# Layer norms in two passes on VectorE, and an output projection block by block with all weights on chip

## The chip, the core and the metric

One core of a Trainium2 chip runs the kernel. The metric is device time in microseconds, from the median of the runs. A core has TensorE (matmuls and transposes, results in eight PSUM banks), VectorE, ScalarE, GpSimd, and SyncE, whose queue issues all the transfers of this kernel.

## The reference, cut to what matters

One layer over 1024 tokens of width 1024: a mixer (forgetting attention and a gated linear recurrence, each projected to the full width, gated and added), its output projection, a residual with a layer norm, a SwiGLU FFN of hidden width 2816, and a second residual with a layer norm.

```python
merged = sigmoid(gate_a) * p_a + sigmoid(gate_b) * p_b
mix = merged @ w_o
x = layer_norm(ALPHA * x + mix, ln1_g, ln1_b)
u, g = split(x @ w_ff_in)
x = layer_norm(ALPHA * x + (silu(g) * u) @ w_ff_out, ln2_g, ln2_b)
# layer_norm(x, g, b) = (x - mean) * rsqrt(var + eps) * g + b, all in float32
```

## The kernel before, in words

Every float32 operand of a large matmul is split in two parts, high (`act.copy`, a cast on ScalarE) and low (`dve.tensor_sub` on VectorE; `split`), and `mm3` makes three matmuls of a product: high x high, high x low, low x high. A stationary tile has 128 x 128 elements, a moving one 128 x 512.

*The order of the work.* No engine's order is written by hand. Every call is first put down by `Plan.add`, with what it reads and writes; `Plan.schedule` then walks through time with a table of costs (`cost`, `LAT`), and gives each free engine the call that can start first, among equals the one with the lowest rank (the order of the calls; `plan.early` lowers a rank by `EARLY` = 3000). `issue` emits that order. A tile of a tag takes one of the tag's `BUFS` buffers as soon as one is free, in the order of first use (tags in `LOOSE` in any order). So each engine runs a fixed queue that was worked out from costs, and a call that comes late on the chip holds up what is queued behind it.

*Buffers.* `x`: five of 16 KB a partition (first the input, then the merged activations `mh`, `ml` of both token halves, then FFN operands). `wr0`, `wr1`: one raw weight load each, used in turn. `wh0`, `wl0`, `wh1`, `wl1`: two each, for split weights. `kb`, `pf`: four each (`REST` is these eight). `ph`, `tt`: four, `gt`: two, all of 512 elements a partition.

*Merge.* For each of 8 column blocks the second branch's product (banks `pps`) is gated, added, and split into `mh`, `ml`.

*Output projection.* The first 512 output columns go over all 8 token blocks at once, in eight banks (`o_acc`), one contraction row c after the other, with weights as they come. Then `z[t] = ALPHA * x + acc`, and the weights of the other 512 columns (`wo1`) are split into `REST`. For these, each token block t has its 24 matmuls (bank `o`), eviction, statistics (`stats`), and its layer norm.

*Layer norm* (`layer_norm`, `affine`). Mean and variance from `bn_aggr`; `rstd` by a power on GpSimd; `nmr` on VectorE; one pass a half on ScalarE (z * rstd + nmr); then the multiplication by g and the addition of b, on the engines that `engs` names ("d" VectorE, "p" GpSimd): "dp" in the first norm, "pp" and "dp" in the second. Only the very last block has its norm in two VectorE passes a half, in the branch `st is not None`.

*Transposes.* Eight transposes a block (`x1t`) make the FFN's operands X11, X12 (blocks 0 to 3) and X22, with copies r1, r2 (blocks 4 to 7).

*FFN.* Both products are formed from seven products of quarter matrices (p1 to p7; Winograd's form), on sums of operands: S1 to S4 on the token side, made by VectorE and ScalarE from r1 and r2 after the loop over blocks, and sums of weight quarters (`Chunk.sums`). Chunks 0 and 1 go product by product together (banks fa to fd), since S1 to S4 are made meanwhile; from chunk 2 on each goes by itself. Raw weights of a chunk come into `pf`.

*Second FFN product.* Six products over all groups, then p3 token block by token block, with its `ds` groups (weights `dbp`, activations `dap`, split into `dp`) kept on chip. Blocks 4 to 7 are complete after p7 and are normed beside p2; blocks 0 to 3 after p3.

Of the kernel before, what the change touches and what calls it, by code (L numbers as in the profile page):

```python
# [283 lines left out]
def trunk(ctx: ExitStack, tc, a: dict, out: bass.AP):  # L284
# [568 lines left out]
    def layer_norm(t, gb, engs, st=None, out=None):  # L853
# [6 lines left out]
        if st is not None:  # L860
            for hf in range(2):
                zt = z[t][:, hs(hf)]
                dve.scalar_tensor_tensor(zt, zt, mv[:, 0:1], gb[0][hf], op0=ALU.subtract, op1=ALU.mult)
            for hf in range(2):
                zt = z[t][:, hs(hf)]
                dve.scalar_tensor_tensor(zt, zt, rstd, gb[1][hf], op0=ALU.mult, op1=ALU.add)
                if out is not None:
                    sync.dma_start(out[:, hs(hf)], zt)
            return None
        nmr = small([P, 1], "nmr")  # L870
        dve.tensor_scalar(nmr, mv[:, 0:1], rstd, -1.0, op0=ALU.mult, op1=ALU.mult)
        for hf in range(2):
            zt = z[t][:, hs(hf)]
            act.activation(zt, zt, AF.Identity, bias=nmr, scale=rstd)
        return lambda: affine(t, gb, engs, out)

    def affine(t, gb, engs, out):
        for hf in range(2):
            zt = z[t][:, hs(hf)]
            e = [dve if x == "d" else pool for x in engs]  # L880
            e[0].tensor_mul(zt, zt, gb[0][hf])
            e[1].tensor_add(zt, zt, gb[1][hf])
            if out is not None:
                sync.dma_start(out[:, hs(hf)], zt)

    acc = [bank(ALL[t], f"o_acc{t}") for t in range(NT)]
    for c2 in range(KC // 2):
        w = weights(a["w_o"][0, c2], [2, NB], f"wo{c2}")
        for j in range(2):
            c = 2 * c2 + j  # L890
            for t in range(NT):
                lh, ll = mtok(t, c)
                mm3(acc[t], lh, ll, *w[j], c == 0, c == KC - 1)
    for t in range(NT):
        zt = z[t][:, hs(0)]
        dve.scalar_tensor_tensor(zt, zt, ALPHA, acc[t], op0=ALU.mult, op1=ALU.add)
    wo1 = []
    for c2 in range(KC // 2):
        raw = raw_load(a["w_o"][1, c2], [2, NB], f"wo1_{c2}")
        wo1.append([take(REST[2 * c2 + j], [2, NB], f"wo1{'hl'[j]}{c2}", F32R) for j in range(2)])  # L900
# [400 lines left out]
```

## Time and profile before

| | us |
|---|---|
| median of 3 runs | 1496.17 (1495.97 to 1496.75) |
| profiled execution, its own time | 1496.65 |
| its span, first to last instruction | 1494.9 |
| TensorE busy in the span | 1470.2 (98%) |
| VectorE busy | 998.2 (67%) |
| ScalarE busy | 671.5 (45%) |
| GpSimd busy | 156.2 (10%) |
| mean granted TensorE clock | 0.995 of full |

The profile is one execution recorded on the chip. Times in it are us from the start of the span, means of a group are in ns. A row of a timeline gives start, duration, engine, line, operation, output <- inputs, and in brackets how long the engine was idle before it and what ended that. Since all calls are emitted from one place, every row has line L280, and a reader goes by the names of the tiles. Matmuls are pipelined: a 512 wide one shows 0.39 us, while the next starts 0.23 us after it. PE is TensorE, PEld its weight loads, DVE VectorE, ACT ScalarE, POOL GpSimd, SPq SyncE's queue. The granted clock of 1.00 is TensorE's upper level (2.4 GHz), 0.50 its lower one (1.2 GHz).

### The profile page before, as it was taken

The numbers are of one execution on the slowest core, as the hardware profiler recorded it, in microseconds if no ns is written. First come the engines' busy times: TensorE is split into PE (matmuls) and PEld (weight loads), VectorE is DVE, ScalarE is ACT, GpSimd is POOL, SyncE is SP. The second block draws the span as 40 slices with busy tenths as digits, with TensorE's granted clock in tenths as the row PEclk, the third lists the DMA queues.
The fourth block names the chain that finished last, engine by engine and source line by source line (L and its number), as shares of the span: only waits on it lengthen the run. The fifth ranks groups of instructions, "written<-read, shape, count | busy, mean of one in ns | idle before, by whom it ended". The sixth has DMA issues, their size and how long they took to land.

```text
span 1494.9 us, 19370 instructions
## 1 busy us (share of the span) xinstructions
PE 1470.2 (98%) x7081; PEld 1218.2 (81%) x7081; DVE 998.2 (67%) x1890; ACT 671.5 (45%) x1133; POOL 156.2 (10%) x156
## 2 busy tenths in 40 slices
PE   9999999999999999999999899999999999999997
PEld 7987888888888888888887678888888888888885
DVE  5148676677797871135827998766666666798594
ACT  5127666677667743234512543332333333534341
POOL 0004132120100000000003300000000000000075
PEclk9999999999999999999999999999999999999998
DMA  7202212121211214347520124332232326977631
GB/s 245 73 29 83 75 47 78 54 60 40 82 37 52 78 59 154 106 163 255 182 69 0 57 86 136 101 100 97 98 100 101 102 104 200 338 271 242 225 118 71
DMA packets 78414, 170.67 MB, mean 114 GB/s; under 512 B 7400, under 2 KB 20328, under 8 KB 78320
## 3 DMA queue, kind: packets, MB, share of 16 engines
q1 hardware_dynamic: 78320, 169.44, 33.9%
q8 instruction: 56, 0.92, 0.2%
q14 instruction: 38, 0.31, 0.1%
HBM read 130.32 MB, written 39.09 MB: 113 GB/s over the span
## 4 chain that ended last, share of the span: by engine, by line
PE 72%; issue 17%; DVE 6%; POOL 2%; ACT 1%; DMA 0%; DVEq 0%; POOLq 0%; ACTq 0%
PE fb L280 12%; PE p L280 12%; PE fc L280 8%; PE fa L280 8%; PE bps L280 8%; PE gps L280 5%; PE va_acc L280 3%; PE vb_acc L280 3%; PE kps L280 3%; PE pv L280 2%; PE qps L280 2%; PE pt L280 2%; PE s L280 2%; POOL z L280 2%; PE lp L280 1%
## 5 line engine op out<-in xcount | busy, mean ns | idle before, releaser
L280 PE MATMUL p<-dp 128*128 128x512 f32 (+1 forms) x957 | 212.1, 384 | 3.9 <-DVE dp L280 3.9
L280 PEld LDWEIGHTS p<-dp 128*128 128x128 f32 x957 | 176.2, 189 | 39.9 <-DVE dp L280 4.2
L280 PE MATMUL fb<-xs,Tp 128*128 128x512 f32 x528 | 127.2, 389 | 0.7 <-DVE xs L280 0.4
L280 PE MATMUL fc<-xs,Tp 128*128 128x512 f32 x528 | 127.6, 389 | 0.0
L280 PE MATMUL fa<-x,Tp 128*128 128x512 f32 x504 | 122.2, 390 | 0.7 <-ACT p L280 0.7
L280 PEld LDWEIGHTS fb<-xs,Tp 128*128 128x128 f32 x528 | 98.9, 188 | 22.0 <-DVE xs L280 0.9
L280 PEld LDWEIGHTS fc<-xs,Tp 128*128 128x128 f32 x528 | 99.1, 188 | 21.0 <-ACT Tp L280 0.4
L280 PEld LDWEIGHTS fa<-x,Tp 128*128 128x128 f32 x504 | 94.6, 188 | 20.7 <-ACT p L280 1.2
L280 ACT CAST Tp<-t 128x512 fp32r<-128x512 f32 x88 | 54.2, 620 | 113.9 <-PE fc L280 65.6
L280 PE MATMUL gps<-xl,wg_h 128*128 128x512 f32 x256 | 101.3, 396 | 0.0
L280 PE MATMUL gps<-xh,wg_h 128*128 128x512 f32 x256 | 101.2, 395 | 0.0
L280 DVE TENSOR_TENSOR Tp<-t,Tp 128x512 fp32r<-128x512 f32 x88 | 60.7, 690 | 60.3 <-ACT Tp L280 59.9
L280 PE MATMUL gps<-xh,wg_l 128*128 128x512 f32 x256 | 100.7, 394 | 0.0
L280 POOL TENSOR_TENSOR rstd<-ve,mhalf 128x1 f32<-128x1 f32 x16 | 11.7, 730 | 825.0 <-DVE ve L280 824.0
L280 ACT CAST dp<-dap 128x1024 fp32r<-128x1024 f32 (+1 forms) x42 | 41.1, 982 | 90.9 <-PE p L280 40.3
L280 PE MATMUL bps<-xh,wb_l 128*128 128x512 f32 x192 | 76.0, 397 | 0.0
L280 PE MATMUL bps<-xh,wb_h 128*128 128x512 f32 x192 | 75.9, 396 | 0.0
L280 PE MATMUL bps<-xl,wb_h 128*128 128x512 f32 x192 | 75.9, 395 | 0.0
L280 DVE TENSOR_TENSOR tl<-pt,th 128x512 fp32r<-128x512 f32 (+1 forms) x96 | 50.7, 552 | 20.3 <-ACT th L280 20.0
L280 DVE TENSOR_TENSOR dp<-dap,dp 128x1024 fp32r<-128x1024 f32 (+1 forms) x42 | 51.8, 1235 | 16.1 <-ACT dp L280 16.0
L280 POOL TENSOR_SCALAR p<-p,rs 128x128 f32<-128x128 f32 (+3 forms) x64 | 47.8, 753 | 140.5 <-DVE rs L280 92.0
L280 DVE TENSOR_TENSOR wg_l<-wg_r,wg_h 128x512 fp32r<-128x512 f32 x32 | 22.5, 703 | 57.6 <-ACT wg_h L280 57.6
(287 smaller groups left out, 3414.1 us busy)
## 6 DMA issues: line engine op xcount, KB each, us to landing
dbp<-in_w_fo SPq DMA_DIRECT2D x45, 512.0 KB, 5.2
dap<-a_d SPq DMA_DIRECT2D x35, 512.0 KB, 4.7
wu_r<-in_w_ff SPq DMA_DIRECT2D x22, 512.0 KB, 3.6
wg_r<-in_w_ff SPq DMA_DIRECT2D x22, 512.0 KB, 3.5
a_d<-ar SPq DMA_DIRECT2D x42, 256.0 KB, 3.4
a_d<-as SPq DMA_DIRECT2D x33, 256.0 KB, 2.8
wg_r<-in_w_g SPq DMA_DIRECT2D x16, 512.0 KB, 3.7
gate_d<-gt SPq DMA_DIRECT2D x32, 256.0 KB, 2.4
```

What stands on the lines that cost most here:

```text
L280: getattr(q.engine, method)(*args, **kw)
```

## The change

The form of layer norm that the last block had becomes the only one: (z - mean) * g, then * rstd + b, four SCALAR_TENSOR_TENSOR a block on VectorE; ScalarE and GpSimd (but for the power) no longer take part. The output projection takes both column halves of a token block together: all weights `wo` of both halves are loaded and split at its start (rows 0 and 1 into the fifth `x` buffer, 2 and 3 into `wh`/`wl`, the rest into `REST`); blocks 0 to 2 run together, row by row, in six banks, and blocks 3 to 7 one after the other, half by half. The sums for S1 and the updates of r1, r2 move into the loop over blocks (for block 7 behind it). The raw weights of chunks 0 and 1 load into an `x` buffer instead of `pf`; their first two products have rank `EARLY`. The second norm's statistics get a tile of their own.

```diff
--- before
+++ after
@@ -850,58 +850,51 @@
     def stats(t, hf):
         dve.bn_stats(lnst[:, t, hf, :], z[t][:, hs(hf)])
 
-    def layer_norm(t, gb, engs, st=None, out=None):
+    def layer_norm(t, gb, st=None, out=None):
         mv = small([P, 2], "mv")
         dve.bn_aggr(mv, (lnst[:, t] if st is None else st).rearrange("p a b -> p (a b)"))
         ve = small([P, 1], "ve")
         dve.tensor_scalar(ve, mv[:, 1:2], LN_EPS, None, op0=ALU.add)
         rstd = small([P, 1], "rstd")
         pool.tensor_tensor(rstd, ve, mhalf[:, :1], op=ALU.pow)
-        if st is not None:
-            for hf in range(2):
-                zt = z[t][:, hs(hf)]
-                dve.scalar_tensor_tensor(zt, zt, mv[:, 0:1], gb[0][hf], op0=ALU.subtract, op1=ALU.mult)
-            for hf in range(2):
-                zt = z[t][:, hs(hf)]
-                dve.scalar_tensor_tensor(zt, zt, rstd, gb[1][hf], op0=ALU.mult, op1=ALU.add)
-                if out is not None:
-                    sync.dma_start(out[:, hs(hf)], zt)
-            return None
-        nmr = small([P, 1], "nmr")
-        dve.tensor_scalar(nmr, mv[:, 0:1], rstd, -1.0, op0=ALU.mult, op1=ALU.mult)
         for hf in range(2):
             zt = z[t][:, hs(hf)]
-            act.activation(zt, zt, AF.Identity, bias=nmr, scale=rstd)
-        return lambda: affine(t, gb, engs, out)
-
-    def affine(t, gb, engs, out):
+            dve.scalar_tensor_tensor(zt, zt, mv[:, 0:1], gb[0][hf], op0=ALU.subtract, op1=ALU.mult)
         for hf in range(2):
             zt = z[t][:, hs(hf)]
-            e = [dve if x == "d" else pool for x in engs]
-            e[0].tensor_mul(zt, zt, gb[0][hf])
-            e[1].tensor_add(zt, zt, gb[1][hf])
+            dve.scalar_tensor_tensor(zt, zt, rstd, gb[1][hf], op0=ALU.mult, op1=ALU.add)
             if out is not None:
                 sync.dma_start(out[:, hs(hf)], zt)
 
-    acc = [bank(ALL[t], f"o_acc{t}") for t in range(NT)]
-    for c2 in range(KC // 2):
-        w = weights(a["w_o"][0, c2], [2, NB], f"wo{c2}")
+
+    gb1 = lnrow("ln1_g", "ln1_b")
+    wo = {}
+
+    def wo_load(hf, c2, hi, lo):
+        raw = raw_load(a["w_o"][hf, c2], [2, NB], f"wo{hf}_{c2}")
+        if isinstance(hi, list):
+            for j in range(2):
+                split(hi[j], lo[j], raw[:, j])
+        else:
+            split(hi, lo, raw)
         for j in range(2):
-            c = 2 * c2 + j
-            for t in range(NT):
-                lh, ll = mtok(t, c)
-                mm3(acc[t], lh, ll, *w[j], c == 0, c == KC - 1)
-    for t in range(NT):
-        zt = z[t][:, hs(0)]
-        dve.scalar_tensor_tensor(zt, zt, ALPHA, acc[t], op0=ALU.mult, op1=ALU.add)
-    wo1 = []
-    for c2 in range(KC // 2):
-        raw = raw_load(a["w_o"][1, c2], [2, NB], f"wo1_{c2}")
-        wo1.append([take(REST[2 * c2 + j], [2, NB], f"wo1{'hl'[j]}{c2}", F32R) for j in range(2)])
-        split(*wo1[c2], raw)
-    for t in range(NT):
-        stats(t, 0)
-    gb1 = lnrow("ln1_g", "ln1_b")
+            wo[hf, 2 * c2 + j] = tuple(x[j] if isinstance(x, list) else x[:, j] for x in (hi, lo))
+
+    wx = take("x", [4, 2, NB], "wox", F32R)
+    for hf in range(2):
+        wo_load(hf, 0, wx[:, 2 * hf], wx[:, 2 * hf + 1])
+    for hf in range(2):
+        wo_load(hf, 1, *([half(f"w{x}{hf}", f"wo{hf}_{x}{j}", F32R) for j in range(2)] for x in "hl"))
+    for c2 in range(2, KC // 2):
+        for hf in range(2):
+            wo_load(hf, c2, *(take(REST[4 * c2 + 2 * hf + j - 8], [2, NB], f"wo{hf}_{'hl'[j]}{c2}", F32R)
+                              for j in range(2)))
+    OTAGS = ("s", "s", "s", "h", "h", "pv")
+    accs = [[bank(OTAGS[(2 * t + hf) % 6], f"o{hf}_{t}") for hf in range(2)] for t in range(NT)]
+
+    def wo_mm(t, hf, c):
+        lh, ll = mtok(t, c)
+        mm3(accs[t][hf], lh, ll, *wo[hf, c], c == 0, c == KC - 1)
 
 
 
@@ -917,14 +910,20 @@
         return ap.rearrange("p (c t) -> p c t", t=P)
 
     for t in range(NT):
-        o = bank("gh"[t % 2], f"o1_{t}")
-        for c in range(KC):
-            lh, ll = mtok(t, c)
-            mm3(o, lh, ll, wo1[c // 2][0][:, c % 2, :], wo1[c // 2][1][:, c % 2, :], c == 0, c == KC - 1)
-        zt = z[t][:, hs(1)]
-        dve.scalar_tensor_tensor(zt, zt, ALPHA, o, op0=ALU.mult, op1=ALU.add)
-        stats(t, 1)
-        layer_norm(t, gb1, "dp" if t < NT - 1 else "dd")()
+        if t == 0:
+            for c in range(KC):
+                for i in range(3):
+                    for hf in range(2):
+                        wo_mm(i, hf, c)
+        elif t > 2:
+            for hf in range(2):
+                for c in range(KC):
+                    wo_mm(t, hf, c)
+        for hf in range(2):
+            zt = z[t][:, hs(hf)]
+            dve.scalar_tensor_tensor(zt, zt, ALPHA, accs[t][hf], op0=ALU.mult, op1=ALU.add)
+            stats(t, hf)
+        layer_norm(t, gb1)
         s_ = blk(t % 4)
         tps = []
         for g in range(2):
@@ -938,13 +937,27 @@
         if t < 4:
             continue
         if t == 4:
-            X22 = operand("x", "x22")
+            X22, S1 = operand("x", "x22"), operand("x", "xs1")
             r2s = [take(f"wr{i}", [2, NB], f"r2s{i}") for i in range(2)]
         r1, r2 = (by4(x) for x in (half(("ph", "tt")[t % 2], f"r1_{t}"), r2s[t // 2 - 2][:, t % 2, :]))
         act.copy(r1, tps[0])
         split(X22[0][:, :, s_], X22[1][:, :, s_], tps[1])
         act.copy(r2, tps[1])
+
+        def first_sums(s_=s_, r1=r1, r2=r2, t=t):
+            s1 = by4(half("gt", f"s1r{t}"))
+            dve.tensor_add(s1, r1, r2)
+            split(S1[0][:, :, s_], S1[1][:, :, s_], s1)
+
+        def next_sums(s_=s_, r1=r1, r2=r2):
+            dve.tensor_sub(r1, f(X11[0])[:, :, s_], r1)
+            dve.tensor_add(r1, r1, f(X11[1])[:, :, s_])
+            dve.tensor_sub(r2, r2, r1)
+
         late.append((s_, r1, r2))
+        if t < NT - 1:
+            first_sums()
+            next_sums()
 
 
 
@@ -961,12 +974,15 @@
 
     TSLOTS = ("kb", "kb", "kb", "kb", "wr0", "wr1")
 
-    def stationary(src, name, apart=False):
+    lane01 = [0]
+
+    def stationary(src, name, apart=False, plain=False):
         if apart:
-            hi, lo = (take(f"w{x}0", [4, P], name + x, F32R) for x in "hl")
+            hi, lo = (take(f"w{x}{lane01[0]}", [4, P], name + x, F32R) for x in "hl")
+            lane01[0] ^= 1
         else:
-            t = take(TSLOTS[turns["T"] % len(TSLOTS)], [2, 4, P], name, F32R)
-            turns["T"] += 1
+            t = take("kb" if plain else TSLOTS[turns["T"] % len(TSLOTS)], [2, 4, P], name, F32R)
+            turns["T"] += not plain
             hi, lo = t[:, 0], t[:, 1]
         split(hi, lo, src)
         return hi, lo
@@ -978,9 +994,9 @@
             mm3(o, T[0][:, c], T[1][:, c], A[0][:, c], A[1][:, c], first and c == 0, c == 3, more)
 
     class Chunk:
-        def __init__(self, c):
+        def __init__(self, c, raw=None):
             self.c = c
-            self.g, self.u = (take("pf", [KC, P], f"w{n}{c}_r") for n in "gu")
+            self.g, self.u = raw or (take("pf", [KC, P], f"w{n}{c}_r") for n in "gu")
             for i, t in enumerate((self.u, self.g)):
                 sync.dma_start(t, a["w_ff"][c, i])
             self.r = {}
@@ -994,9 +1010,10 @@
                 dve.tensor_sub(self.r[n], x, y)
 
         def T(self, n, apart=False):
+            plain = self.c < 2
             src = {"p1": self.g[:, :4], "p2": self.g[:, 4:], "p3": self.u[:, 4:], "p4": self.r.get("4"),
                    "p5": self.r.get("1"), "p6": self.r.get("2"), "p7": self.r.get("3")}[n]
-            return stationary(src, f"T{n}_{self.c}", apart)
+            return stationary(src, f"T{n}_{self.c}", apart, plain)
 
     OPS = {"p1": X11, "p2": X12, "p4": X22}
     ars = {}
@@ -1052,32 +1069,30 @@
         activations(c, a0, a1)
 
 
-    ks = [Chunk(c) for c in range(2)]
+    first_sums()
+    plan.early = EARLY
+    raws = take("x", [4, KC, P], "w01_r")
+    ks = [Chunk(c, (raws[:, 2 * c], raws[:, 2 * c + 1])) for c in range(2)]
     banks = [[next_bank(f"f{n}{c}") for n in "abcd"] for c in range(2)]
     for k, o in zip(ks, banks):
         mul(k, "p1", o[0], True, True)
         k.p1 = half("ph", f"p1_{k.c}")
         act.copy(k.p1, o[0])
     for k, o in zip(ks, banks):
-        mul(k, "p2", o[0], False)
+        mul(k, "p2", o[0], False, True)
         k.sl = half("gt", f"sl{k.c}")
         act.activation(k.sl, o[0], AF.Silu)
-    S1 = OPS["p5"] = operand("x", "xs1")
-    for s_, r1, r2 in late:
-        S1r = half("wh1", "s1r")
-        dve.tensor_add(by4(S1r), r1, r2)
-        split(S1[0][:, :, s_], S1[1][:, :, s_], by4(S1r))
+    plan.early = 0
+    OPS["p5"] = S1
     for k, o in zip(ks, banks):
         k.sums("1", "2")
         mul(k, "p5", o[2], True)
         k.sums("4")
         mul(k, "p4", o[3], True)
+    next_sums()
     S3 = OPS["p7"] = operand("x", "xs3")
     S2 = OPS["p6"] = operand("x", "xs2")
     for s_, r1, r2 in late:
-        dve.tensor_sub(r1, f(X11[0])[:, :, s_], r1)
-        dve.tensor_add(r1, r1, f(X11[1])[:, :, s_])
-        dve.tensor_sub(r2, r2, r1)
         split(S2[0][:, :, s_], S2[1][:, :, s_], r2)
     for k, o in zip(ks, banks):
         mul(k, "p6", o[1], True)
@@ -1143,6 +1158,7 @@
     u = [half(("wh0", "wl0", "wh1", "wl1")[i], f"fu{i}") for i in range(4)]
     ai = {"p1": 0, "p5": 1, "p6": 2, "p7": 3, "p4": 4, "p2": 5, "p3": 6}
     gb2 = lnrow("ln2_g", "ln2_b")
+    lnst = take("gt", [NT, 2, 6], "lnst2")
     XS = ("x",) * 5
     for prod in ("p1", "p5", "p6", "p4", "p7", "p2"):
         if prod == "p7":
@@ -1178,14 +1194,13 @@
                 dve.tensor_add(z21, z21, u[t])
                 for hf in range(2):
                     stats(t + 4, hf)
-                layer_norm(t + 4, gb2, "pp", None, out[blk(t + 4), :])()
+                layer_norm(t + 4, gb2, None, out[blk(t + 4), :])
             else:
                 dve.tensor_add(z11, z11, o)
                 if t < 3:
                     stats(t, 0)
     ds = [group("p3", ai["p3"], g) for g in range(len(GR))]
     st = take("gt", [4, 6], "lnst3")
-    before = None
     for t in range(4):
         final = t == 3
         parts = [slice(i * 256, (i + 1) * 256) for i in (2, 3)] if final else [hs(1)]
@@ -1205,10 +1220,7 @@
                 dve.bn_stats(st[:, 2 + i, :], z[t][:, s_])
         if not final:
             stats(t, 1)
-        after = layer_norm(t, gb2, "pp" if t < 2 else "dp", st if final else None, out[blk(t), :])
-        if before:
-            before()
-        before = after
+        layer_norm(t, gb2, st if final else None, out[blk(t), :])
     plan.issue(SLACK, SWITCH)
```

## Rows read from the trace of the kernel before

**Rows 1.** The page's busy time of each engine: us, share of the span, instructions.
```profile
PE 1470.2 (98%) x7081; PEld 1218.2 (81%) x7081; DVE 998.2 (67%) x1890; ACT 671.5 (45%) x1133; POOL 156.2 (10%) x156
```

**Rows 2.** Busy time of each engine by stretch, then TensorE's clock, DMA share, GB/s.
```profile
400.00:500.00 100.00, 97.51 (x515) 81.71 (x513) 82.35 (x169) 67.26 (x105) 6.16 (x5) 1.00 0.18 56
...
790.00:840.00 50.00, 48.59 (x230) 37.69 (x229) 36.73 (x69) 18.35 (x29) 21.54 (x18) 1.00 0.01 2
840.00:860.00 20.00, 14.18 (x56) 10.67 (x55) 19.66 (x34) 14.65 (x24) 4.95 (x4) 0.83 0.28 104
860.00:880.00 20.00, 19.30 (x84) 15.33 (x84) 20.00 (x34) 8.95 (x16) 0.00 (x0) 1.00 0.17 53
...
1420.00:1495.00 75.00, 63.91 (x305) 53.32 (x303) 55.33 (x82) 21.49 (x27) 48.42 (x34) 0.94 0.28 95
```

**Rows 3.** List of TensorE's waits: us in total, times, longest us.
```profile
PE x1t L280 <- POOL z L280: 6.2, 6, 5.0
...
PE ot L280 <- DVE ob L280: 1.6, 1, 1.6
```

**Rows 4.** TensorE in order of time, the two large gaps.
```profile
845.44 1.11 PE L280 MATMUL x1t<-ident,z 128*128 128x128 f32 x4 [5.02 <-POOL z L280]
...
1462.80 25.06 PE L280 MATMUL p<-dp 128*128 128x512 f32 x134 [3.93 <-DVE dp L280]
```

**Rows 5.** Stretches of 2 us behind the two gaps, columns as in rows 2.
```profile
846.00:848.00 2.00, 2.00 (x9) 1.42 (x7) 2.00 (x4) 1.41 (x3) 1.21 (x2) 0.50 0.10 37
848.00:850.00 2.00, 1.92 (x6) 1.39 (x5) 2.00 (x5) 1.76 (x4) 0.69 (x1) 0.50 0.00 0
850.00:852.00 2.00, 2.00 (x7) 1.49 (x6) 2.00 (x5) 1.55 (x3) 0.00 (x0) 0.63 0.00 0
852.00:854.00 2.00, 1.27 (x8) 0.84 (x7) 2.00 (x5) 1.11 (x2) 0.00 (x0) 1.00 0.02 4
...
1462.00:1464.00 2.00, 1.20 (x3) 1.01 (x4) 1.41 (x4) 0.00 (x0) 0.16 (x1) 0.61 0.60 223
```

**Rows 6.** SyncE's queue, ScalarE and GpSimd in order of time, first gap.
```profile
839.33 0.37 SPq L280 DMA_DIRECT2D wg_r<-in_w_ff  x1
...
843.63 0.62 ACT L280 CAST Tp_0h<-wg_r 128x512 fp32r<-128x512 f32 x1 [0.82 <-DMA wg_r<-in_w_ff]
...
843.79 3.27 POOL L280 TENSOR_TENSOR z<-z,ln_b 128x512 f32<-128x512 f32 x2 [2.85 <-issue]
```

**Rows 7.** GpSimd, ScalarE and VectorE in order of time, second gap.
```profile
1453.95 1.53 POOL L280 TENSOR_TENSOR rstd<-ve,mhalf 128x1 f32<-128x1 f32 x1
...
1455.76 1.52 ACT L280 ACTIVATE z<-z,nmr,rstd 128x512 f32<-128x512 f32 x2 [10.31 <-DVE nmr L280]
...
1462.07 0.68 DVE L280 TENSOR_TENSOR dp<-dbp,dp 128x512 fp32r<-128x512 f32 x1
```

**Rows 8.** The chain that ended last, one product of a chunk (start, us).
```profile
970.09 2.72 PE fb L280 x12
```

**Rows 9.** VectorE in order of time: passes in a run, in the tail, a split.
```profile
785.00 3.66 DVE L280 SCALAR_TENSOR_TENSOR z<-z,o_acc 128x512 f32<-128x512 f32 x6
...
1394.43 1.22 DVE L280 TENSOR_TENSOR dp<-dbp,dp 128x1024 fp32r<-128x1024 f32 x1
...
1490.51 1.41 DVE L280 SCALAR_TENSOR_TENSOR z<-z,rstd,ln_b 128x512 f32<-128x512 f32 x2
```

**Rows 10.** ScalarE in order of time, two casts of projection weights.
```profile
760.06 1.05 ACT L280 CAST wo1h<-wo_r 128x1024 fp32r<-128x1024 f32 x1 [4.20 <-DMA wo_r<-in_w_o]
...
765.90 1.05 ACT L280 CAST wo1h<-wo_r 128x1024 fp32r<-128x1024 f32 x1 [4.27 <-DMA wo_r<-in_w_o]
```

**Rows 11.** VectorE's groups from 1419.6 to 1463.5: busy us, mean ns.
```profile
L280 DVE TENSOR_TENSOR dp<-dbp,dp 128x1024 fp32r<-128x1024 f32 (+1 forms) x7 | 12.1, 1726 | 0.0
L280 DVE TENSOR_TENSOR dp<-dap,dp 128x1024 fp32r<-128x1024 f32 (+1 forms) x7 | 11.8, 1689 | 0.4 <-ACT dp L280 0.4
```

## Prediction

> **What bounds the kernel now.** I read the engines' busy shares first. TensorE is busy in 1470.2 of the span's 1494.9 us [rows 1], so nothing that the change does on other engines counts unless it ends an idle gap of TensorE or a stretch at the low clock. The busy time by stage [rows 2] says where those are: 790 to 840 (48.59 of 50 us busy), 840 to 860 (14.18 of 20, mean clock 0.83), 860 to 880 (19.30 of 20), and 1420 to 1495 (63.91 of 75, clock 0.94). The list of waits names them [rows 3]: transposes x1t waiting for GpSimd's z, then a 1.6 us wait of another stage (ot, in the stretch from 400 to 500) that the change doesn't touch.
>
> The two large gaps, in order of time on TensorE [rows 4]: 5.02 us before the transposes at 845.44, and 3.93 us before the matmuls at 1462.80. After each the granted clock lies at the lower level (1.2 GHz, 0.50 in the rows) for some us before it is full again [rows 5]. That is the whole stock from which the change can gain.
>
> **First gap (end of the output projection, start of the FFN).** The transposes of block 6 wait for GpSimd's `z<-z,ln_b`, which starts only at 843.79 and takes 3.27 us for two; the FFN's first weights, issued at 839.33, land at 843.63, where ScalarE's cast begins [rows 6]. So two things are late by nearly the same time, and removing one alone shows the other. Cost of the stretch: 5.02 us idle, 0.73 us idle at 852 to 854 (1.27 of 2 busy), and the busy time below full clock, 2.00 x 0.50 + 1.92 x 0.50 + 2.00 x 0.37 = 2.7 us [rows 5]: 8.45 us.
>
> **Second gap (last product of the FFN).** ScalarE's two passes of `z<-z,nmr,rstd` for block 7 stand in its queue after an idle time of 10.31 us, waiting for a rstd that GpSimd delivers at 1453.95 + 1.53, behind its own `ln_g` and `ln_b` passes; behind them stand the casts of the last weight group, and VectorE's subtraction for it comes at 1462.07 [rows 7]. Cost: 3.93 us idle; then 134 matmuls in 25.06 us [rows 4]. By the code 66 of these are 256 wide and 68 are 512 wide; with 2.72 us for 12 wide ones [rows 8], 0.227 each, and half of that for the narrow ones, they would need 15.4 + 7.5 + 0.2 = 23.1. So 2.0 us went to the low clock: 5.9 us in all.
>
> **The change, part by part.**
>
> *Number of matmuls.* 8 blocks x 2 halves x 8 x 3 = 384 before and after, same shapes: 0.
>
> *Layer norm.* It removes from each of the 16 blocks (15; the last has the new form already) two ScalarE passes, the small `nmr`, and two multiplications and two additions that GpSimd and VectorE shared; it puts four SCALAR_TENSOR_TENSOR on VectorE. One of these costs 0.60 us in a run of six (3.66 us) and 0.70 in the tail (1.41 us for two) [rows 9]; I take 0.65. A block's norm then costs VectorE 2.6 us, where it paid 1.2 with the pair "d" and "p", and 0 with "pp".
>
> *Projection block.* For a block after the fourth VectorE has two evictions, two statistics, four norm passes, one low part of X22 and now the sums for S1 and r1, r2 in the loop (five): 10 x 0.60 + 4 x 0.65 = 8.6 us, plus 0.3 of small ones. TensorE spends 48 x 0.227 = 10.9 us on it, transposes left out. VectorE keeps up with 2 us to spare a block; in 790 to 840 it had 36.73 of 50 [rows 2]. The first three blocks finish together after 144 matmuls, 32.6 us; their norms (some 19 us) have the 22 us of blocks 3 and 4 as cover. If that cover were too short, transposes would be late, not the projection itself, since six banks rotate. I take half of the 1.4 us idle in 790 to 840 as gained (bounds 0 and 1.4): -0.7.
>
> *Weights on chip.* All 4 MB go through the same two raw buffers. A pair of halves (1 MB) serves 36 matmuls, 8.16 us. Before, two of its loads follow each other at 5.84 us, cast to cast [rows 10]; I read them as two rounds of one buffer, so with two buffers a pair comes every 5.9 us or so: it fits. The four loads of the norm's rows now stand ahead of them on SyncE's queue and cost the first pair time, not the later ones. At the start both halves of the first pair are wanted, where before one was; the second can go behind work on the first half. I take 0.3 us lost (bounds 0 and 2).
>
> *Start of the FFN.* Its first two chunks now load into an x buffer, the one that held projection rows 0 and 1. The splits go into buffers of projection weights that were read earlier still. The x buffer's last reader is block 7, second half, row 1; after it come 6 x 3 matmuls, 4.1 us. With E the end of the projection the loads go out at E - 3.9. The gate half is the second issued, 0.43 us later, and landed 4.3 us after its issue before [rows 6]: E + 0.8; cast 0.62 and semaphore: first matmul at E + 1.6, and 0.3 lost on the low part. Block 6's norm no longer waits for GpSimd: its transposes fall ahead of E. Chunk 1's weights come some 3 us after chunk 0's, which cover 2.7: 0.6 more. Remaining loss 2.5 us, a gap of about 1.6, after which I expect no fall of the clock: the 1.6 us wait of ot [rows 3] lies in a stretch whose mean clock is 1.00 [rows 2]. Next come p1 and p2 of both chunks, 48 matmuls or 10.9 us, which need nothing of block 7; its norm (evict, statistics, aggregate, GpSimd's power, pass: about 5 us) and the last part of S1 (4 more) are ready by E + 10. Gain 8.45 - 2.5 = 5.9. Bounds: 1.0 remaining (gain 7.4), or 8.3 (gain 0.1, first rival).
>
> *Sums moved into the loop.* VectorE is less behind at 860 to 880: of 0.7 us idle there 0.5 gained (0 to 0.7). S4 now takes the buffer of the raw weights, which are read until the last split of chunks 0 and 1, one product ahead of its use: 0.2 lost (0 to 1).
>
> *Last product.* On VectorE 1419.6 to 1463.5 the fourteen splits took 12.1 + 11.8 us, beside GpSimd's passes [rows 11]. Without GpSimd beside it a wide split takes 1.22 alone [rows 9] and by the step of narrow ones some 1.14 in a run, a narrow one 0.60: ten and four make 13.8, ten less. Sixteen norm passes add 10.4, and the additions beside them, slowed in the same way, give some 2 us back. So VectorE's load is about 1.5 us lower, not much; but ScalarE's queue no longer holds a norm, and the order, worked out with costs that GpSimd no longer upsets, can put block 1's matmuls ahead of a late group. Remaining loss 0.6, gain 5.3. Bounds: all 5.9, or 0.9 (second rival).
>
> The Trainium skill speaks against this part: "VectorE: DVE Perf Modes", section on the TRN2 errata, gives an fp32 two-input operation of 512 elements 691 ns, and its rules for authors ask for a low count of operations on this engine. The trace agrees on the single duration (0.70 in the tail [rows 9]), not on a run, where the step is 0.60. By 0.69 for each of the some 47 narrow operations of this stage VectorE would end 4 us later than by 0.60, which is the second rival's way.
>
> *Sum.* 0.7 - 0.3 + 5.9 + 0.5 - 0.2 + 5.3 = 11.9 us off the profiled execution's own 1496.65 (span and 1.75 around it): 1484.7. That execution lies 0.5 above the median of the runs, so 1484.3.
>
> **Rivals.** (1) *The weights take the norm's place.* If the buffer comes free only at E, the gate half lands at E + 4.9 and the first matmul comes at E + 5.6, and the clock falls as it did: 8.3 us remain of 8.45. For it: weights and norm were late by the same time before. Against: the 18 matmuls after the last reader. Gain 11.9 - 5.8 = 6.1: 1490.1. (2) *VectorE full at the end.* If the order of TensorE is kept and VectorE works off evictions and norms first, the last group is split at about 1461 instead of 1462.7: 3 us idle and 2 us of clock remain. Gain 11.9 - 4.4 = 7.5: 1488.7. (3) *Both*: gain 1.7, 1494.5, no measurable change. (4) *Slower: weights late inside the projection.* If one raw buffer's round takes c instead of 5.84, three rounds stall by 3 x (c - 8.16); from c = 12.1 the whole gain is gone, at 14 it is 17.5 us: 1501.8. For it: both buffers now load at once, behind the norm's rows in the queue, and casts share ScalarE with the merge. Against: the needed doubling; the channels are nearly idle there.
>
> **How the numbers follow.** Forecast 0.54; (1) 0.20, (2) 0.13, (3) 0.06, (4) 0.07. A change of 0.2% (3 us) is about what can be told from none. Faster: 0.54 + 0.20 + 0.13 = 0.87; same 0.06; slower 0.07. Range: all bounds at their best, 1.4 + 7.4 + 0.7 + 5.9 = 15.4 gained, give 1480.8; with the rest of the small losses under overlapping matmuls I go to 1479.5. Above it takes in (1) and (2) with the small terms at their worst: 1491.5.
>
> **What would show it.** No GpSimd pass over z, ScalarE free of z; splits of 1.2 us near 1440; TensorE's gap at the end of the projection under 2 us, ended by ScalarE's cast of the first weights and not by z, clock 1.00 after it; no gap above 1 us in the last product; 384 projection matmuls in about 87 us plus transposes. Wrong it would be by a gap of 5 us before the first `fa`, a fall of the clock there, `wo` casts waiting for DMA with TensorE behind them, or VectorE without a pause from the last product on.

## Result and the profile after

The changed kernel takes 1484.29 us (median of 4 runs, 1483.40 to 1484.93); the kernel before, on the same chip, 1496.29 (4 runs). The ratio is 0.9919, 95% interval 0.9902 to 0.9936: faster by 0.8%. The profiled execution took 1483.79 us, with a span of 1482.0, 12.9 less than the span before (the medians are 12.0 apart: this execution lies 0.5 below its median, that of before lay 0.4 above). The forecast was 1484.3. The sum is right; of its terms two are not, in opposite directions, and the page alone doesn't show that.

The page's busy times, to be read against [rows 1]:

```profile
PE 1464.2 (99%) x7081; PEld 1218.4 (82%) x7081; DVE 1005.8 (68%) x1913; ACT 648.7 (44%) x1101; POOL 95.6 (6%) x116
```

The norms' work left GpSimd (156.2 to 95.6 us) and ScalarE (671.5 to 648.7) and cost VectorE only 7.6 us, although it took over 60 passes; the last section says why. TensorE issues the same 7081 matmuls and transposes.

By stretch, columns as in [rows 2] (the whole kernel lies some us earlier from 840 on, so stretches correspond only roughly):

```profile
790.00:840.00 50.00, 47.52 (x230) 39.41 (x228) 41.85 (x73) 11.15 (x19) 4.70 (x5) 1.00 0.13 47
840.00:860.00 20.00, 17.79 (x73) 14.06 (x74) 18.76 (x34) 12.54 (x22) 0.92 (x1) 0.91 0.23 94
860.00:880.00 20.00, 20.00 (x90) 16.58 (x89) 18.67 (x31) 8.18 (x14) 0.00 (x0) 1.00 0.00 1
1420.00:1450.00 30.00, 30.00 (x134) 24.87 (x133) 30.00 (x48) 9.48 (x10) 2.75 (x3) 1.00 0.40 140
```

The waits of TensorE: the 6.2 us behind GpSimd's z of [rows 3] are gone, and first in the list now stands ScalarE's cast of the first FFN weights.

```profile
PE fa L280 <- ACT Tp_0h L280: 4.1, 1, 4.1
PE ot L280 <- DVE ob L280: 1.6, 1, 1.6
```

TensorE in order of time, where [rows 4] had the two gaps. The projection's last matmul starts at 837.14; the first one of the FFN comes 4.11 us after it has ended. The last product runs without a gap: one group, 45.24 us.

```profile
837.14 0.39 PE L280 MATMUL o<-wo_h,ml 128*128 128x512 f32 x1
841.63 1.22 PE L280 MATMUL fa<-x,Tp_0h 128*128 128x512 f32 x2 [4.11 <-ACT Tp_0h L280]
...
1429.73 45.24 PE L280 MATMUL p<-dp 128*128 128x512 f32 x230
```

Behind the gap the clock falls to the lower level, as in [rows 5], but for a shorter time:

```profile
840.00:842.00 2.00, 0.37 (x1) 0.37 (x2) 1.11 (x4) 1.04 (x2) 0.00 (x0) 0.84 1.01 414
842.00:844.00 2.00, 2.00 (x6) 1.48 (x6) 2.00 (x5) 1.62 (x4) 0.89 (x1) 0.50 1.02 418
844.00:846.00 2.00, 2.00 (x9) 1.55 (x8) 2.00 (x4) 0.65 (x2) 0.03 (x1) 0.81 0.27 109
846.00:848.00 2.00, 1.77 (x10) 1.35 (x9) 2.00 (x5) 1.63 (x3) 0.00 (x0) 1.00 0.00 0
```

What was late there, in the terms of [rows 6]: SyncE's queue and ScalarE's cast.

```profile
831.92 0.33 SPq L280 DMA_DIRECT2D wu_r<-in_w_ff  x1
832.36 0.69 SPq L280 DMA_DIRECT2D wg_r<-in_w_ff  x1
833.48 1.99 SPq L280 DMA_DIRECT2D w_r<-in_w_ff  x4
...
840.96 1.14 ACT L280 CAST Tp_0h<-w_r 128x512 fp32r<-128x512 f32 x2 [1.97 <-DMA w_r<-in_w_ff]
```

The issues of the DMAs in 828 to 846 (KB each, median us to landing):

```profile
w_r<-in_w_ff SPq DMA_DIRECT2D x4, 512.0 KB, 7.5
```

The first chunks' loads (w_r) go out at 833.48, 3.9 us before E = 837.4, the projection's end: as predicted, to a tenth. But the cast waits for them until 840.96. Just ahead of them stand chunk 2's two halves, 1 MB (wu_r, wg_r), and the DMA engines are busy without a break (share 1.01 and 1.02 in 840 to 844, at 414 to 418 GB/s).

The last product on VectorE, against [rows 7] and [rows 11]: a norm pass in a run, and the last wide and narrow splits. The narrow one that [rows 7] has at 1462.07 starts at 1453.16 now, and wide ones take 1.22 where the means of [rows 11], narrow ones counted in, were 1.7.

```profile
1417.63 1.41 DVE L280 SCALAR_TENSOR_TENSOR z<-z,mv,ln_g 128x512 f32<-128x512 f32 x2
...
1451.42 1.22 DVE L280 TENSOR_TENSOR dp<-dbp,dp 128x1024 fp32r<-128x1024 f32 x1
...
1453.16 0.69 DVE L280 TENSOR_TENSOR dp<-dbp,dp 128x512 fp32r<-128x512 f32 x1
```

**Where the 12.9 us come from**, by milestones of TensorE. The projection's first matmul: 744.06 before, 743.84 after (0.2). From it to the start of the projection's last: 95.97 and 93.30 (2.7), though block 6's eight transposes, 8 x 0.0975 = 0.8 us of work, now lie inside it. From there to the first matmul of p, the FFN's second product (1271.85 and 1264.94): 4.0 less. From the first of p to the last matmul (215.8 and 209.8): 6.0 less. Tail: 7.3 both times. 0.2 + 2.7 + 4.0 + 6.0 = 12.9.

### The profile page after: what moved, and what is told of

Read it like the earlier page. It is cut to its first block, busy times and chain, and to the rows that moved or that the text cites. A ratio compares the mean times of both kernels' runs of the same rounds, so it can differ in the third digit from the quotient of the medians.

```text
span 1482.0 us, 19306 instructions
## 1 busy us (share of the span) xinstructions
PE 1464.2 (99%) x7081; PEld 1218.4 (82%) x7081; DVE 1005.8 (68%) x1913; ACT 648.7 (44%) x1101; POOL 95.6 (6%) x116
## 4 chain that ended last, share of the span: by engine, by line
PE 94%; DVE 3%; ACT 1%; DMA 1%; issue 0%; POOL 0%; SPq 0%; DVEq 0%; ACTq 0%
PE p L280 14%; PE fb L280 11%; PE gps L280 11%; PE fc L280 8%; PE fa L280 8%; PE bps L280 8%; PE pps L280 6%; PE o L280 6%; PE vb_acc L280 3%; PE va_acc L280 3%; PE pv L280 2%; PE s L280 2%; PE qps L280 2%; PE kps L280 2%; PE pt L280 2%; PE lp L280 1%
## 5 line engine op out<-in xcount | busy, mean ns | idle before, releaser
L280 PE MATMUL fa<-x,Tp 128*128 128x512 f32 x480 | 115.8, 390 | 0.3 <-DVE u L280 0.3
L280 PEld LDWEIGHTS fa<-x,Tp 128*128 128x128 f32 x480 | 90.1, 188 | 19.3 <-ACT p L280 0.7
L280 DVE TENSOR_TENSOR dp<-dap,dp 128x1024 fp32r<-128x1024 f32 (+1 forms) x42 | 47.5, 1133 | 15.2 <-ACT dp L280 15.2
L280 PE MATMUL fb<-x,Tp 128*128 128x512 f32 x240 | 57.7, 389 | 0.0
```

Source lines behind the costliest of these rows:

```text
L280: getattr(q.engine, method)(*args, **kw)
```

## Experiments

Theory at the start: the norms that leave GpSimd carry the gain, at both gaps, and what is left at the start of the FFN is lost to weights that land late behind chunk 2's. Rival: the projection's new arrangement carries it. Ratios below are to the kernel before, run beside it on the same chip.

**1. The two-pass norm alone** in the kernel before (its projection and weights as they were):

```diff
-        if st is not None:
...
-        nmr = small([P, 1], "nmr")
-        dve.tensor_scalar(nmr, mv[:, 0:1], rstd, -1.0, op0=ALU.mult, op1=ALU.mult)
         for hf in range(2):
             zt = z[t][:, hs(hf)]
-            act.activation(zt, zt, AF.Identity, bias=nmr, scale=rstd)
...
+            dve.scalar_tensor_tensor(zt, zt, mv[:, 0:1], gb[0][hf], op0=ALU.subtract, op1=ALU.mult)
         for hf in range(2):
             zt = z[t][:, hs(hf)]
+            dve.scalar_tensor_tensor(zt, zt, rstd, gb[1][hf], op0=ALU.mult, op1=ALU.add)
```

> The kernel before with the two-pass norm alone; projection, sums and weight buffers as they were. Theory (the norm carries the gain): the gap of 3.93 us in the last product and its low clock are gone (-6), the projection block is some 3 us shorter because no transposes wait for GpSimd, and the start of the FFN still waits for its weights, issued when the projection's buffers come free: 1485 to 1488 us. Rival (the block by block projection carries what was won before the second FFN product): only the last product gains, 1490 us or more.

Measured: 1487.29 us, ratio 0.9938 (0.9922 to 0.9955). The projection ends 4.3 us earlier than before, the last product has no gap, and TensorE's first FFN matmul shows what the norm had covered, the weights:

```profile
836.17 1.33 PE L280 MATMUL x1t<-ident,z 128*128 128x128 f32 x8
840.31 0.73 PE L280 MATMUL fa<-x,Tp_0h 128*128 128x512 f32 x2 [2.81 <-ACT Tp_0h L280]
```

The norm alone gives 9.0 of the 12 us. By the milestones used above, the projection is 3.5 us shorter (92.4 from its first matmul to its last), the last product 6.0, and the stretch between them 1.1 longer (432.9 instead of 431.8). So at the first gap the norm alone gains nothing: waits for the weights and for later operands (Tp, xs) take the old wait's place, and the clock is low there too (0.50 in 842 to 846). The theory above, which had the norm pay at both gaps, fell in that part.

**2. The rest of the change with the old norm** (the changed kernel, with the three-step norm of before put back where it is used):

```diff
-        layer_norm(t, gb1)
+        layer_norm(t, gb1, "dp" if t < NT - 1 else "dd")()
...
-                layer_norm(t + 4, gb2, None, out[blk(t + 4), :])
+                layer_norm(t + 4, gb2, "pp", None, out[blk(t + 4), :])()
```

> The changed kernel with the old norm (ScalarE, GpSimd and VectorE passes), everything else as changed. Theory (the norm carries the gain): GpSimd's passes over z are back, so the transposes wait again and the last product has its gap of about 4 us: 1493 to 1498 us. Rival (the projection carries half of it): the gap of the last product is back, the rest stays, 1490 us.

Measured: 1496.92 us, 1.0003 (0.9993 to 1.0012): nothing. The last product has its wait of 3.9 us back, and the projection is full of small waits for GpSimd:

```profile
PE p L280 <- DVE dp L280: 3.9, 1, 3.9
PE fa L280 <- ACT p L280: 2.5, 2, 1.8
PE fa L280 <- ACT Tp_0h L280: 2.2, 1, 2.2
PE x1t L280 <- POOL z L280: 1.9, 5, 0.6
```

Yet on top of the new norm the same edit is worth 1487.3 - 1484.3 = 3.0 us (medians of two sets of runs, whose kernels before agree to 0.01). In the profiled executions, whose spans differ by 3.8, it lies between the projection's last matmul and the first of p: 432.9 us with the norm alone, 427.8 with both (0.8 of the 5.1 is eight transposes, which now run in the projection). The parts don't add: this one pays only once the norm is out of its way.

**3. Only the last product's four norms off GpSimd** (the kernel before; the multiplication and addition go to VectorE, ScalarE keeps its pass):

```diff
-                layer_norm(t + 4, gb2, "pp", None, out[blk(t + 4), :])()
+                layer_norm(t + 4, gb2, "dd", None, out[blk(t + 4), :])()
```

> The kernel before, with only the four norms behind p7 changed: multiplication and addition on VectorE instead of GpSimd, ScalarE's pass kept. Theory (GpSimd's passes delay the fourth rstd, and ScalarE waits for it in front of the last casts): the gap of 3.93 us falls below 1 us, 1490 to 1491 us. Rival (any norm pass in ScalarE's queue holds the casts up, and VectorE is full): a gap of 2 to 4 us stays, 1494 to 1497 us.

Measured: 1490.41 us, 0.9960 (0.9946 to 0.9975). The gap of 3.93 us [rows 4] is gone and the other one stays:

```profile
PE x1t L280 <- POOL z L280: 6.2, 6, 5.0
PE ot L280 <- DVE ob L280: 1.6, 1, 1.6
```

This one word gives 5.9 us, the whole loss that the prediction had worked out for that gap. ScalarE's pass is still there, so the cause was not that pass but GpSimd's: by holding back rstd, and with it ScalarE's queue, or by slowing the splits on VectorE. No run parts these two, but the trace of the kernel before weighs them. Beside GpSimd's passes, from 1437 to 1455, eight wide splits took 2.2 to 2.3 us each; without them, in this experiment, wide ones take 1.2. And ScalarE's last cast had ended at 1458.31, 3.8 us ahead of VectorE's split at 1462.07 [rows 7]; from 1419.61 to that split VectorE waited only 0.44 us for rstd and 0.37 for ScalarE. So the slowed splits weigh more than the queue. VectorE and ScalarE before, then VectorE in this experiment:

```profile
1448.30 2.31 DVE L280 TENSOR_TENSOR dp<-dap,dp 128x1024 fp32r<-128x1024 f32 x1
...
1457.70 0.61 ACT L280 CAST dp<-dbp 128x512 fp32r<-128x512 f32 x1
```

```profile
1448.52 1.22 DVE L280 TENSOR_TENSOR dp<-dbp,dp 128x1024 fp32r<-128x1024 f32 x1
```

**4. Chunk 2's loads behind the first chunks'** (the changed kernel; chunk 2's raw weights get buffers that the projection reads later):

```diff
-            wo_load(hf, c2, *(take(REST[4 * c2 + 2 * hf + j - 8], [2, NB], f"wo{hf}_{'hl'[j]}{c2}", F32R)
+            wo_load(hf, c2, *(take(REST[4 * hf + 2 * c2 + j - 4], [2, NB], f"wo{hf}_{'hl'[j]}{c2}", F32R)
```

> The changed kernel with the projection weights of the two halves placed in the eight buffers by half, so that chunk 2's raw weights can't load before the projection's last 18 matmuls. Theory (1 MB for chunk 2 stands ahead of the first chunks' weights on the queue and delays them by about 3 us): the first gate half lands 3 us earlier, the gap in front of the FFN falls from 4.1 to about 1.2 us, the clock stays full, 1479 to 1481 us. Rival (the four loads share the channels and land together some 7 us after issue whatever is ahead): gap and time as they are, 1483 to 1485 us.

Measured: 1481.70 us, 0.9902 (0.9888 to 0.9917), 2.6 less than the changed kernel. SyncE's queue and ScalarE:

```profile
833.33 1.75 SPq L280 DMA_DIRECT2D w_r<-in_w_ff  x4
835.86 0.33 SPq L280 DMA_DIRECT2D wu_r<-in_w_ff  x1
...
838.23 1.14 ACT L280 CAST Tp_0h<-w_r 128x512 fp32r<-128x512 f32 x2
```

The loads go out when they do in the changed kernel (833.48 there), and the cast no longer waits for them: it starts 4.9 us after the first issue instead of 7.5. So the 1 MB ahead of them was the delay. The gap is 1.5 us and the clock stays at 1.00 through it. The time is 0.7 above what was expected: the waits of the FFN's matmuls for ScalarE's copies of p1 are 1.7 us in all, where they were 0.6. The planner's order behind the gap differs in a few places too, so not all of the 2.6 need be the loads'.

**5. The gate halves of both chunks first** (the changed kernel):

```diff
+    for i in (1, 0):
+        for k in ks:
+            sync.dma_start((k.u, k.g)[i], a["w_ff"][k.c, i])
```

> The changed kernel with the loads of the first two chunks in the order gate, gate, up, up instead of up, gate, up, gate; chunk 2's loads still stand ahead. Theory (loads land in the order of issue, 1.3 to 1.5 us each): the first gate half lands some 1.4 us earlier and the second some 2.8, the gap falls from 4.1 to about 2.7 us, 1481 to 1483 us. Rival (the four share the channels and land together): gap and time as they are, within 1 us of 1484.3.

Measured: 1484.86 us, 0.9922 (0.9907 to 0.9936). The cast starts at 839.98 instead of 840.96 and the gap is 2.88 us instead of 4.11, but waits of 1.6 us for ScalarE's r and 1.4 for its copies of p1 follow it, and nothing is gained. The wait had moved as the theory said; the time is that of the rival.

**6. The moved sums, put back behind the loop** (the changed kernel):

```diff
-        if t < NT - 1:
-            first_sums()
-            next_sums()
+        sums.append((first_sums, next_sums))
...
-    first_sums()
+    for x in sums:
+        x[0]()
```

> The changed kernel with the sums for S1 and the updates of r1 and r2 behind the loop over blocks again. Theory (VectorE, which now carries the norms, is behind at the start of the FFN, and the sums in the loop relieve it by fifteen operations, 9 us): TensorE waits for Tp and xs in p5 to p7 for some 3 us, 1487 to 1488 us. Rival (as forecast, where 0.5 us was put to this part): 1484 to 1485 us.

Measured: 1484.74 us, 0.9919 (0.9904 to 0.9934). The expected 1487 to 1488 didn't come, but neither is the theory tested: by the trace, every engine and SyncE's queue have the same instructions in the same order as in the changed kernel. It is the planner that sets VectorE's order, and the place in the loop is no matter to it. So this run shows what one order of work does from one execution to another: the gap before the FFN was 3.72 us here and 4.11 there, the median time 0.45 us apart.

**7. Block 7 reads rows 0 and 1 of both halves first** (the changed kernel), so that the x buffer comes free some 4 us earlier; and, as a further one, this together with experiment 5:

```diff
-            for hf in range(2):
-                for c in range(KC):
-                    wo_mm(t, hf, c)
+            n = 2 if t == NT - 1 else KC
+            for c0, c1 in ((0, n), (n, KC)):
+                for hf in range(2):
+                    for c in range(c0, c1):
+                        wo_mm(t, hf, c)
```

> The changed kernel, but block 7 of the projection takes rows 0 and 1 of both halves first, so that the x buffer for the first chunks' weights comes free 36 matmuls (8.2 us) before the end instead of 18 (4.1 us), and ahead of chunk 2's buffers. Theory (the gap in front of the FFN is the landing of these loads and nothing else): the first gate half lands 3 us or more before the projection's end, the gap of 4.1 us is gone, the clock stays full, 1476 to 1479 us. Rival (block 7's norm, or VectorE's queue, is late next and takes the gap's place): a gap of 2 us or more stays, ended by z or by the low part, 1481 to 1484 us.

> Both together: rows 0 and 1 first in block 7, and gate halves loaded first. Theory: the loads are early enough already, so that the order among them adds little; 1476 to 1479 us, within 1 us of the kernel with the rows alone. Rival (chunk 1's weights are the next wait): 1 to 2 us below it.

Measured: 1483.51 us (0.9911, 0.9896 to 0.9925) and 1483.56 (0.9911, 0.9895 to 0.9928). The loads went out at 829.01 and the first cast began at 833.84, yet the theory's 1476 to 1479 fell; the time is the rival's, though the wait is neither for z nor for a low part. The order of the loads adds nothing on top, as expected. The early rank of p1 and p2 drew chunk 0's p1 into the projection, and chunk 0's p2 then waited for a copy of p1. That copy stood in ScalarE's queue behind four casts, the first of which could start only with the projection's end, at 840.59, and then waited 0.86 us itself for a subtraction on VectorE (`xs<-r,xs`):

```profile
840.39 0.39 PE L280 MATMUL o<-wo_h,ml 128*128 128x512 f32 x1
844.27 1.02 PE L280 MATMUL fa<-x,Tp_0h 128*128 128x512 f32 x2 [3.49 <-ACT p L280]
```

**8. Without that rank**: as 7, with p1 and p2 of the first two chunks in their plain place; and as a further one with the loads in the order of experiment 4 too:

```diff
     first_sums()
-    plan.early = EARLY
```

> As rows_early (block 7 takes rows 0 and 1 of both halves first, so that the x buffer comes free 8 us before the projection's end), and the first two chunks' p1 and p2 no longer get the early rank. Theory (what ate the gain of rows_early was the order: p1 of chunk 0 drawn into the projection, its copy then queued late on ScalarE, and p2 of chunk 0 held TensorE for 3.5 us): with p1 behind the projection the gap before the first fa is at most 1 us and the clock does not fall; 1478 to 1481.5. Rival (the weights' arrival was never what counts once it is under 5 us; chunk 1's weights and the splits on VectorE, in their fixed order, lose the same 3 to 4 us wherever p1 stands): 1483 to 1485, with a wait for a split or a copy of 2 us or more within 10 us of the projection's end.

> rows_noearly with the loads in the order of pf_late (chunk 2's 1 MB behind the first chunks' loads). Theory: chunk 1's weights come earlier too, nothing of the start of the FFN waits for a load any more; 1477 to 1480, at least 1 us under pf_late. Rival (in pf_late the loads were already early enough; what is left there are the copies and splits on ScalarE and VectorE): 1481 to 1483, the same as pf_late.

Measured: 1479.62 us (0.9887, 0.9872 to 0.9902) and 1480.47 (0.9890, 0.9873 to 0.9906). The first is the fastest kernel of this study. Its first FFN matmul follows the projection without a gap, as the theory asked. The second was expected at least 1 us under experiment 4 and is 1.2 under it by the medians (the intervals overlap) and 0.5 above its own range; against the first it is no faster. Both run the same instructions in the same order on every engine and on SyncE's queue. With the x buffer free this early the first chunks' loads go out first in both (828.50 and 828.25); only chunk 2's go out later in the second (835.78 instead of 833.33), and that gains nothing. One large wait is left in both, 1.90 us for the copy of p1; here TensorE, ScalarE and VectorE of the first:

```profile
842.58 0.73 PE L280 MATMUL fa<-x,Tp_0h 128*128 128x512 f32 x2 [1.90 <-ACT p L280]
...
841.94 0.58 ACT L280 COPY p<-fa 128x512 f32<-128x512 f32 x1 [2.41 <-DVE z L280]
...
841.11 1.40 DVE L280 SCALAR_TENSOR_TENSOR z<-z,mv,ln_g 128x512 f32<-128x512 f32 x2
```

A copy of p1 that waits for z looks odd, until one asks whose buffer p1 gets. By the code it is the next of four halves of one pool, two of which hold the norm's gain; the first pass over it, half of the two in the last line, ends at about 841.8.

**9. The norm's rows in each other's buffers**, everything else as in 8:

```diff
-        for name, tag in ((gname, "ph"), (bname, "tt")):
+        for name, tag in zip((gname, bname), ("tt", "ph") if gname == "ln1_g" else ("ph", "tt")):
```

> As rows_noearly, with the first norm's rows in each other's buffers: the gain in the two that held the offset, the offset in the two that held the gain, of which the first chunk's p1 takes the first. Theory (the 1.9 us for which TensorE waits there for the copy of p1 are the copy waiting for the last reader of the gain's buffer, block 7's first norm pass, which ends at 841.8, just before the copy at 841.94): the copy now waits for the pass with the offset, which ended 1.3 us later or more; the wait grows to 3 to 4 us, and the time by 1.3 to 3 us, to 1481 to 1483. Rival (the copy stands behind the casts in ScalarE's queue, or the accumulation is read late; the buffer is no matter): the wait stays at 1.9 and the time at 1479 to 1480.5.

Measured: 1480.81 us, 0.9900 (0.9883 to 0.9916). The copy moved from behind the pass with the gain to behind the pass with the offset, 1.27 us later, as the theory said; ScalarE and VectorE:

```profile
843.21 0.58 ACT L280 COPY p<-fa 128x512 f32<-128x512 f32 x1 [3.30 <-DVE z L280]
...
842.37 1.41 DVE L280 SCALAR_TENSOR_TENSOR z<-z,rstd,ln_b 128x512 f32<-128x512 f32 x2
```

So the buffer sets the wait. The time is 1.2 us longer by the medians and 0.0013 by the ratio (the intervals overlap), and 0.2 below the expected range: the planner put eight transposes first behind the gap, which is 2.58 us long, not 3 to 4.

## Why the prediction was right, and where it was not

**Right total, with one failed step.** The step that failed is in the start of the FFN: "The gate half is the second issued, 0.43 us later, and landed 4.3 us after its issue before [rows 6]: E + 0.8". The issue came at E - 3.9 as predicted, but the cast could start only at E + 3.6 and the first matmul came at E + 4.3 instead of E + 1.6. The 4.3 us had been measured on a load with only the up half of its own chunk, 0.5 MB, just ahead of it; the change also frees chunk 2's buffers 1.5 us earlier, and 1 MB more goes out first. Experiment 4 shows this: with that order turned round the cast starts 2.6 us sooner after the issue, and 2.6 us come off the time. The prediction looked at when the buffer comes free and at the order on its own queue position, not at what else the change frees just before it. The words "after which I expect no fall of the clock" went with it: the gap was 4.11 us, not 1.6.

In the prediction's own way of counting, the stretch now loses 4.11 idle, 0.23 idle at 846 to 848 and 2.00 x 0.50 + 2.00 x 0.19 + 0.37 x 0.16 = 1.4 at the lower clock: 5.8 us of the former 8.45. The gain is 2.7, where 5.9 was forecast and its bounds were 0.1 and 7.4. It lies half-way between the forecast and the first rival. Nor is it the norm's gain alone, as the prediction's "Block 6's norm no longer waits for GpSimd" may suggest: with the norm alone the stretch from the projection to p grew by 1.1 us (experiment 1).

**Undersized: the projection block.** 0.7 - 0.3 was forecast for it with its weights; it gave 2.7, and 3.5 with the eight transposes that it now holds besides. The 1.4 us of idle time that the prediction halved is what the busy time shows. TensorE's records overlap: a wide matmul is drawn 0.39 us long and the next starts 0.227 after it, so a delay of 0.16 us shows as no idle time, and one of 0.5 as 0.34. By starts, less 0.227 for each matmul and 0.0975 for each transpose, the projection before lost 4.3 us, after 0.9; the largest were 0.3 to 0.5 each before transposes that waited for GpSimd's z. Experiments 1 and 2 agree: by the same count the norm alone leaves 0.8 us lost (it ends the projection 4.3 us earlier, but 0.7 of that lies ahead of its first matmul), and the new arrangement with the old norm loses 5.6. So this gain is the norm's, not the arrangement's. No `wo` cast had TensorE wait, so the fourth rival (weights late inside the projection) didn't come.

**Nearly right: the last product.** 5.3 forecast, 6.0 measured from the first of p to the end, 5.5 so counted in experiment 3. The 0.6 us that was to remain didn't: no gap at all. VectorE is indeed busy without a pause from 1412.7 to 1454.5, the second rival's sign, but two things close the gap, and the prediction named both. VectorE's load fell: its last split ends 188.9 us after the first of p, where it ended 190.9 after it (2.0 less; 1.5 forecast). And the planner put more of block 1's matmuls ahead of the late group: 134 of p came behind that split, now 123. What weighed less than the prediction had it is the norm in ScalarE's queue (experiment 3). The Trainium skill, "VectorE: DVE Perf Modes", section on the TRN2 errata, spoke against this part with 691 ns for an fp32 operation of two inputs; the trace has that for a single one (0.69) and 0.60 for the step between narrow splits (1452.56 to 1453.16), as before, and 0.66 for a norm pass (1417.63 to 1418.95 for two). The prediction's 0.65 holds.

**Small terms.** Sums moved into the loop: 0.5 forecast. The stretch 860 to 880 did lose its 0.7 us of idle time [rows 2], but the place of the sums in the code can't be what did it (experiment 6: same order of work, 20.00 of 20 busy); what did was not tried. S4's new buffer caused no wait in the list.

**The sum.** Forecast 0.4 + 5.9 + 0.3 + 5.3 = 11.9; measured 3.5 + 2.7 + 0.5 + 6.0 and 0.2 ahead of all = 12.9 of span (the 0.5 is what is left of the 4.0 between the projection and p, less the eight transposes and the 2.7). An error of -3.2 at the start of the FFN was made up by +3.1 in the projection and +0.7 at the end. That the forecast met the median so closely is luck. What was right is that the norm on VectorE ends the gap in the last product, and that what remains at the first gap is a wait for the weights.

## What to carry to other kernels

When a change frees several buffers at nearly the same time, write down every load that this releases, in the order of release, and price the one you need behind all that go out before it: here 1 MB ahead cost 2.6 us and a fall of the clock. When a wait ends "by" something that the instruction doesn't read, ask whose buffer it writes. Measure a stage's loss by the starts of its matmuls, not by idle time, when records overlap. And where a planner sets the order, look in the trace whether an edit changed that order before you read its time (experiment 6).

## What the runs showed of the hardware that was not expected

After the gaps of 4.11 us (the changed kernel), 3.49 (experiment 7) and 2.81 (experiment 1) the granted clock fell to 0.50 or 0.51, the lower level; after the 1.5 us of experiment 4 it stayed at 1.00. The length of a gap doesn't decide alone. The two kernels of experiment 8 have TensorE's instructions in the same order, and both wait 1.90 us at the same place. In the first the clock stayed full, in the second (second line) it fell:

```profile
844.00:846.00 2.00, 2.00 (x12) 1.69 (x12) 2.00 (x4) 1.98 (x4) 0.00 (x0) 1.00 0.00 0
```

```profile
844.00:846.00 2.00, 2.00 (x8) 1.75 (x7) 2.00 (x5) 1.88 (x4) 0.00 (x0) 0.50 0.00 0
```

In experiment 9 a gap of 2.58 us was followed by 1.00, in experiment 2 one of 2.17 by 0.50. One profile of each was taken, so how often it goes either way is open.

GpSimd and VectorE slow each other, and the prediction allowed for that in the last product alone. Where both worked without a pause before, a wide split took 2.31 us instead of 1.22 (experiment 3), and two GpSimd passes took 4.5 us (at 1445.01 and 1449.49) instead of 2.5 (at 1467.71 and 1476.16). GpSimd's small power for rstd took 0.55 us in nine of sixteen cases before and 1.53 beside wide splits [rows 7]; it takes 0.91 to 0.99 in fifteen of sixteen now, beside VectorE's norm passes, so that its mean rose from 730 to 914 ns. VectorE's groups of splits over the whole span, busy us and mean ns:

```profile
L280 DVE TENSOR_TENSOR dp<-dap,dp 128x1024 fp32r<-128x1024 f32 (+1 forms) x42 | 47.5, 1133 | 15.2 <-ACT dp L280 15.2
...
L280 DVE TENSOR_TENSOR dp<-dbp,dp 128x1024 fp32r<-128x1024 f32 (+1 forms) x24 | 27.1, 1129 | 1.9 <-ACT dp L280 1.9
```

Before, they took 51.8 and 31.7 us, so 8.9 more for the same 66 instructions. By the same view the 60 new norm passes add 42.4 us to VectorE, and the 35 operations that they replace there (15 small nmr, 20 wide ones) had taken 17.5. That would be 24.9 more; the total rose by 7.6. Work that VectorE had done all along became 17.3 us shorter: these 8.9, 2.0 in the additions `z<-z,fu` beside them (the prediction had ten and two), 3.7 in the sums and low parts at the start of the FFN, and the rest in small amounts.
